# Sixteen expert items instead of seventeen: one item holds three experts

## The chip, the cores and the metric

One Trainium2 chip, one of its cores. A TensorE does matrix products of up to 128 x 128 weights against up to 512 columns; VectorE, ScalarE (ACT) and GpSimd (POOL) work on rows of 128 partitions; SyncE (SP) issues the loads of weights. The metric is the device time of one execution in microseconds (us), the median of several runs.

## The reference, cut to what matters

Two transformer blocks behind each other, for 512 tokens of 1024 values. The first has attention and a convolution, an output projection, and then a mixture of experts; the second (stick-breaking attention, gated linear attention, a gated mixer, a feed-forward layer) follows. The expert part is what changes:

```python
g_logits = hf @ w_rg + b_rg                    # 4 groups: top 1
e_logits = (hf @ w_re + b_re).reshape(T, 4, 8) # 8 experts in the group: top 2
eid = grp[:, None] * 8 + top_idx               # 512 tokens x 2 = 1024 assignments to 32 experts
y = (silu(x @ w_gate[e]) * (x @ w_up[e])) @ w_down[e]   # 1024 -> 512 -> 1024, fp32
out[token] += weight * y
```

All 32 experts' weights (6.3 MB each, 201 MB in all) have to be read; how many tokens an expert has depends on the data. The mixer of the second block ends in `mix @ w_o` with an RMS norm behind it (a sum of squares over 1024 channels), and the router stands behind another RMS norm.

## The kernel before, in words

**Expert items.** The experts are worked off in items of up to 128 token slots. An item's token rows are gathered by a product with a one-hot matrix (lines 1142 to 1195; `oh` on VectorE, `psg` on TensorE, high and low part of the rows, 64 products for two items at a time), then go through gate, up and down (`gate_up`, `down`), and a product with a second one-hot matrix adds the result to the tokens (`scatter`, line 1294). Fifteen items are pairs: two experts with 64 slots each, whose two products of 64 columns of weights run in the two halves of TensorE's array (`both`, line 1201). The expert with the most tokens (HOT) has an item to itself with 128 slots, and so has expert 31 (LAST). The list is `items = [*range(8), LAST, *range(8, NPR - 1), HOT, NPR - 1]`, 17 items. LAST is gathered by itself with 128 columns; HOT is gathered together with the pair at place 14. An expert with more tokens than slots would send the rest to a loop behind the items (line 1419), which runs as often as there are such blocks.

**Order.** From the second item on the order of TensorE's products is that of the program (`fixed`, line 1130). In each item: half of the gate, the transposes of the item before (`hidden_T`), half of the gather for the next two items where it is due, the second half of the gate, the down products of the item before, the second half of the gather, then up with the scatter of the item before in between (from line 1371 on). Before that, and around item 0, a scheduler places the instructions.

**The route.** Behind the router's logits VectorE finds each token's experts. `slots` (line 1048) counts the tokens of each expert, picks HOT and exchanges its place with that of expert 30, finds each assignment's slot (`sid`) and writes the list of experts by place (`ovf`). A table of tokens and weights by slot follows (`tsl`, `wsl`, by products `pstab`). Items 0 and 1 hold experts 0 to 3, whatever the data (`NFX = 4`), with slots found ahead of all this (`sid0`), so their gather and weights need not wait.

**Loads.** A stream issues loads of 1 MB on SyncE in the order of use, into 15 buffers in four pools; a load waits for its buffer. Of the pairs each load holds half for one and half for the other expert. From item 2 on SyncE reads the expert's number from `ovf` first.

**The other places.** The router (line 808) has in each of 8 steps a product for 36 logits and one for the sum of squares; both come between the output projection's products. Behind the items the second block's value projection starts; its weights are split in a high and a low part, the low part of the first two tiles by GpSimd (line 1458). The mixer's output projection (`mix_mm`, `mix_out`, lines 2170 to 2199) has 8 steps of two halves; the sum of squares over channels is a product with ones, one for each step and half (`Sums`, line 1630).

Of the kernel before, what the change touches and what calls it, by code (L numbers as in the profile page):

```python
# [11 lines left out]
F32 = mybir.dt.float32  # L12
# [8 lines left out]
P = 128  # L21
# [13 lines left out]
    ("b_mod", 48), ("g_norm1", 8), ("conv_b", 4), ("conv_ln_g", 4), ("conv_ln_b", 4),  # L35
    ("conv_w", 4 * 31), ("g_norm2", 8), ("w_router", 8 * 36), ("c", 8),
# [162 lines left out]
def _build(ctx, nc, tc, I, out, dbg):  # L199
# [108 lines left out]

    def mm3(ps, lh, ll, rh, rl, first, last):
# [39 lines left out]
    NPR, CAP, NFX = NE // 2 - 1, 64, 4  # L349
    HOT, LAST = NPR, NPR + 1  # L350
# [88 lines left out]
    def W(p, i):  # L439
# [3 lines left out]
        if p == LAST:  # L443
            return I["w_moe"][NE - 1, i]
        if p == HOT:
            return lambda: of(expert(2 * NPR), 1)
        if 2 * p < NFX:
# [3 lines left out]
    items = [*range(8), LAST, *range(8, NPR - 1), HOT, NPR - 1]  # L451

    def add_item(p, part):
        n = 2 if p >= NPR else 4
# [160 lines left out]
    with tc.issue_after(behind.ins):  # L615
# [6 lines left out]
        e64, base0, cand, isl, ish = [h2p.tile([P, NE], F32, name=n) for n in ("e64", "base0", "cand", "isl", "ish")]  # L622
        ts(e64, iota[:, :NE], 64.0, None, OP.mult)
        ts(isl, iota[:, :NE], float(NE - 1), None, OP.is_equal)
        ts(ish, iota[:, :NE], float(NE - 2), None, OP.is_equal)
        stt(base0, isl, 64.0, e64, OP.mult, OP.add)
        ts(cand, iota[:, :NE], NFX - 0.5, -1.0e5, OP.is_le, OP.mult)
        stt(cand, isl, -1.0e5, cand, OP.mult, OP.add)
# [174 lines left out]
    def router(st):  # L803
# [4 lines left out]
        mm(plg[0][0:36, :], wr(m), xs, start=(m == 0), stop=(m == KD - 1), skip_group_check=True)  # L808
        mm(plg[1][64:96, :], ones[:, 0:32], sq, start=(m == 0), stop=(m == KD - 1), skip_group_check=True)
# [146 lines left out]
    ovf = mp.tile([P, NOV + NE], I32, name="ovf")  # L956
# [91 lines left out]
    def slots():  # L1048
# [4 lines left out]
        key, hot, cap, base, ob, d, nb, g = [sm(NE) for _ in range(8)]  # L1053
        mx, at = sm(1), sm(1)
        stt(key, cn, float(NE), cand, OP.mult, OP.add)
        red(mx, key, axis=AX.X, op=OP.max)
        ts(hot, key, mx, None, OP.is_equal)
        tt(cap, hot, isl, OP.add)
        ts(cap, cap, float(CAP), float(CAP), OP.mult, OP.add)
        tt(ob, hot, base0, OP.mult)  # L1060
        nc.vector.reduce_sum(at, ob, axis=AX.X)
        ts(at, at, float(HOT * P), None, OP.subtract)
        stt(base, hot, float(HOT * P), base0, OP.mult, OP.add)
# [1319 lines left out]
```

## Time and profile before

| | |
|---|---|
| three timed runs | 1812.36, 1812.47, 1816.58 us (median 1812.47) |
| profiled execution | 1818.69 us, span 1816.9 us |
| TensorE busy | 1745.1 us (96%) |
| VectorE / ScalarE / GpSimd busy | 881.3 / 629.3 / 109.6 us |
| read from memory | 322.0 MB, 180 GB/s over the span |
| granted clock of TensorE, mean | 0.978 |

A profile shows one execution. Places in it are microseconds from the start of the span. "PE" is TensorE's products, "PEld" its loading of weights. Because products are pipelined, the difference between two starts tells what one costs, and its own duration is longer. fp32 products go in two passes and stand as two instructions.

### The profile page before, as it was taken

How to read it: one execution, taken by the hardware profiler on the slowest of the kernel's cores; microseconds unless marked ns; L12 is line 12 of the kernel's file. 1: busy time of each engine (PE TensorE's matmuls, PEld its weight loads, DVE VectorE, ACT ScalarE, POOL GpSimd, SP SyncE). 2: the span in 40 equal slices, each digit the busy share in tenths (PEclk: the TensorE clock that was granted, in tenths of full speed). 3: DMA queues.
4: the chain of work that ended last, by engine and by line, in shares of the span. 5: the costliest groups of instructions: out<-in, count | busy, mean ns of one | idle time of the engine just before them, and what ended most of it. 6: DMA issues, size and time to landing. Idle time of an engine off the chain costs nothing.

```text
span 1816.9 us, 26870 instructions
## 1 busy us (share of the span) xinstructions
PE 1745.1 (96%) x10826; PEld 1263.2 (70%) x10826; DVE 881.3 (49%) x1597; ACT 629.3 (35%) x1141; POOL 109.6 (6%) x147
## 2 busy tenths in 40 slices
PE   7999997999999999998899999999999999999997
PEld 4776565444445444445788668989999899789985
DVE  6789654433333334235577742253332645335534
ACT  5226653211111111104567743242233633223322
POOL 2000010000000000003200100030000111001101
PEclk9989898999999999999999999999999999999998
DMA  8563253999999999930411012113222222222221
GB/s 327 199 242 136 89 216 130 380 409 409 408 411 360 385 408 410 412 128 27 159 67 49 24 47 93 47 63 128 102 100 87 70 91 78 100 93 93 94 87 64
DMA packets 73986, 328.01 MB, mean 181 GB/s; under 512 B 8019, under 2 KB 8403, under 8 KB 59652
## 3 DMA queue, kind: packets, MB, share of 16 engines
q1 hardware_dynamic: 72608, 320.36, 46.6%
q0 software_dynamic: 1248, 5.91, 0.9%
q8 instruction: 86, 1.41, 0.3%
q14 instruction: 40, 0.33, 0.0%
q10 hardware_dynamic: 4, 0.00, 0.0%
HBM read 321.98 MB, written 4.26 MB: 180 GB/s over the span
## 4 chain that ended last, share of the span: by engine, by line
PE 48%; DVE 3%; ACT 2%; DMA 1%; POOL 1%; issue 1%; DVEq 0%; ACTq 0%; POOLq 0%
PE p L1620 11%; PE pup L2232 7%; PE pq L1598 4%; PE pg L312 2%; PE pg L310 2%; PE pg L311 2%; PE pd L311 2%; PE pd L312 2%; PE pd L310 2%; PE pv L310 1%; PE pv L311 1%; PE pv L312 1%; PE pmix L310 1%; PE psum L1643 1%; PE pmix L312 1%; PE pmix L311 1%
## 5 line engine op out<-in xcount | busy, mean ns | idle before, releaser
L224 DVE TENSOR_TENSOR wsplit<-raw,wsplit 128x1024 fp32r<-128x1024 f32 (+1 forms) x140 | 167.4, 1198 | 250.6 <-ACT wsplit L223 244.7
L223 ACT ACTIVATE wsplit<-raw 128x1024 fp32r<-128x1024 f32 (+1 forms) x144 | 146.8, 1022 | 260.5 <-PE pd L312 76.3
L1206 PE MATMUL pgu<-raw,x 128*64 128x512 f32 x960 | 220.3, 598 | 0.0
L1206 PEld LDWEIGHTS pgu<-raw,x 128*64 128x64 f32 x960 | 64.1, 136 | 119.9 <-issue 106.4
L1299 DVE SCALAR_TENSOR_TENSOR x<-psx,modc,x 128x512 f32<-128x512 f32 x136 | 93.2, 745 | 50.1 <-PE psx L1307 50.0
L1248 DVE SCALAR_TENSOR_TENSOR yl<-pdn,wsl,yh 128x512 fp32r<-128x512 f32 x34 | 25.4, 751 | 178.8 <-ACT yh L1247 178.3
L1206 PE MATMUL pdn<-raw,hT 128*64 128x512 f32 x480 | 105.7, 593 | 0.7 <-ACT hT L1228 0.7
L1228 ACT ACTIVATE hT<-pht 128x512 f32<-128x512 f32 x17 | 10.2, 597 | 232.0 <-PE pht L1222 227.5
L1206 PEld LDWEIGHTS pdn<-raw,hT 128*64 128x64 f32 x480 | 34.5, 137 | 69.1 <-issue 64.4
L647 DVE SCALAR_TENSOR_TENSOR y<-u,cpk,y 128x512 f32<-128x512 f32 x116 | 80.6, 748 | 0.1
L311 PE MATMUL pd<-wsplit,ah 128*128 128x512 f32 x176 | 71.1, 404 | 2.1 <-DVE wsplit L224 2.0
L1168 PE MATMUL psg<-oh,h2h 128*128 128x256 f32 (+1 forms) x288 | 67.8, 292 | 3.1 <-DVE oh L1153 3.1
L1620 PE MATMUL p<-nha,wsplit 128*128 128x258 f32 x384 | 69.0, 293 | 1.3 <-ACT wsplit L223 0.7
L312 PE MATMUL pd<-wsplit,al 128*128 128x512 f32 x176 | 70.1, 398 | 0.0
L310 PE MATMUL pd<-wsplit,ah 128*128 128x512 f32 x176 | 68.9, 397 | 0.9 <-ACT wsplit L223 0.9
L1168 PE MATMUL psg<-oh,h2l 128*128 128x256 f32 (+1 forms) x288 | 65.7, 282 | 0.0
L1620 PE MATMUL p<-nhb,wsplit 128*128 128x258 f32 x384 | 65.6, 283 | 0.0
L2232 PE MATMUL pup<-nha,wsplit 128*128 128x258 f32 x352 | 64.0, 291 | 0.4 <-ACT wsplit L223 0.4
L1306 PE MATMUL psx<-ohT,yh 128*128 128x512 f32 x136 | 59.3, 436 | 5.2 <-ACT wsplit L223 5.1
L2232 PE MATMUL pup<-nhb,wsplit 128*128 128x258 f32 x352 | 63.2, 287 | 0.0
L1168 PEld LDWEIGHTS psg<-oh,h2h 128*128 128x128 f32 x288 | 53.6, 196 | 9.7 <-issue 5.7
L1620 PEld LDWEIGHTS p<-nha,wsplit 128*128 128x128 f32 x384 | 56.2, 195 | 3.0 <-ACT wsplit L223 0.9
(653 smaller groups left out, 3973.5 us busy)
## 6 DMA issues: line engine op xcount, KB each, us to landing
raw<-w_moe SPq DMA_DIRECT2D x312, 512.0 KB, 10.1
raw<-w_moe SPq DMA_DIRECT2D x36, 1024.0 KB, 10.0
raw<-w_ff SPq DMA_DIRECT2D x22, 1024.0 KB, 4.8
raw<-w_mod SPq DMA_DIRECT2D x16, 1024.0 KB, 5.9
raw<-w_qk SPq DMA_DIRECT2D x12, 1024.0 KB, 5.1
raw<-w_v SPq DMA_DIRECT2D x8, 1024.0 KB, 4.9
raw<-w_modk SPq DMA_DIRECT2D x8, 1024.0 KB, 5.2
raw<-w_mg SPq DMA_DIRECT2D x8, 1024.0 KB, 4.9
```

The source lines that it names most:

```text
L223: act(hi, src, AF.Copy)
L224: return sub(lo, src, hi.bitcast(F32), OP.subtract)
L310: mm(ps, lh, rh, start=first, stop=False)
L311: mm(ps, lh, rl, start=False, stop=False)
L312: mm(ps, ll, rh, start=False, stop=last)
L647: tap[0] = stt(y[:, m, :], src, w, y[:, m, :], OP.mult, OP.add)
L1168: fix(mm(ps[k // 2][:, k % 2 * 256:][:, :n], w[i][:, k * P:(k + 1) * P], oh[:, i, :n], start=(i == 0 and w is h2h and k % 2 == 0), stop=(i ...
L1206: fix(mm(ps[s, :], l[:, s], w[:, 2 * b + i, :], start=first, stop=last, skip_group_check=True))
L1299: stt(xT[m], ps, gt2(m), xT[m], OP.mult, OP.add)
L1598: mm(ps[a], l[:, kk, :], r[kk][:, a * HF:(a + 1) * HF], start=(kk == 0 and fl == 0), stop=(kk == k - 1 and fl == 2))
L1620: mm(ps[a], l[:, kk, :], ends(r[kk])[:, a], start=(kk == 0 and fl == 0), stop=(kk == k - 1 and fl == 2))
L2232: mm(ps[:, a, :HC], l[:, kk, :], x[kk][:, o:o + HC], start=(kk == 0 and fl == 0), stop=(kk == KD - 1 and fl == 2))
```

## The change

The list has 16 items: 14 pairs, HOT, and an item TRI with three experts: one with 64 slots and the two emptiest (of those from expert 4 on) with 32 each. TRI's products are four of 32 columns, two of which belong to the expert with 64 slots (`three`); its loads are taken in threes (`several`). HOT and TRI stand one after the other in the middle of the list. `slots` now finds the two emptiest too, and exchanges three experts' places one after another (`trade`), and the list of experts by place is found from the places. With it came: the router's two products are 64 columns wide each (the columns of the packed constants are reordered so that 64 can be read), the low parts of the two value tiles go to VectorE, and in the mixer's projection the squares of six steps are added up on VectorE ahead of one product.

```diff
-    NPR, CAP, NFX = NE // 2 - 1, 64, 4
-    HOT, LAST = NPR, NPR + 1
+    NPR, CAP, NFX = NE // 2 - 2, 64, 4
+    HOT, TRI = NPR, NPR + 1
@@ W
+        if p == TRI:
+            e, i = 2 * NPR + 1 + i % 3, i // 3
+            return lambda: of(expert(e), 1)
-    items = [*range(8), LAST, *range(8, NPR - 1), HOT, NPR - 1]
+    items = [*range(8), HOT, TRI, *range(8, NPR)]
@@ router
-        mm(plg[0][0:36, :], wr(m), xs, start=(m == 0), stop=(m == KD - 1), skip_group_check=True)
-        mm(plg[1][64:96, :], ones[:, 0:32], sq, start=(m == 0), stop=(m == KD - 1), skip_group_check=True)
+        mm(plg[0][0:64, :], cc("w_router", 36 * m, 64), xs, start=(m == 0), stop=(m == KD - 1), skip_group_check=True)
+        mm(plg[1][64:128, :], ones[:, 0:64], sq, start=(m == 0), stop=(m == KD - 1), skip_group_check=True)
@@ slots
+        def best(oh, k):
+            mx = sm(1)
+            red(mx, k, axis=AX.X, op=OP.max)
+            ts(oh, k, mx, None, OP.is_equal)
+        def trade(oh, place):
+            at, to = sm(1), sm(1)
+            tt(t, oh, pos, OP.mult)
+            nc.vector.reduce_sum(at, t, axis=AX.X)
+            ts(at, at, float(place), None, OP.subtract)
+            ts(to, at, -1.0, None, OP.mult)
+            ts(t, pos, float(place), None, OP.is_equal)
+            stt(pos, t, at, pos, OP.mult, OP.add)
+            stt(pos, oh, to, pos, OP.mult, OP.add)
         stt(key, cn, float(NE), cand, OP.mult, OP.add)
+        best(hot, key)
+        stt(key, cn, -float(NE), cand, OP.mult, OP.add)
+        stt(key, hot, -1.0e5, key, OP.mult, OP.add)
+        best(c1, key)
+        stt(key, c1, -1.0e5, key, OP.mult, OP.add)
+        best(c2, key)
+        copy(pos, iota[:, :NE])
+        for oh_, place in ((hot, 2 * NPR), (c1, NE - 2), (c2, NE - 1)):
+            trade(oh_, place)
...
-        ts(eo[:, NOV + 1:], base[:, :NE - 1], 1.0 / 64, None, OP.mult)
+        for n, tag in enumerate(("hs", "hT")):
+            at = scratch(tag, DE, NE // 2, NE)
+            tt(at, iota[:, n * NE // 2:][:, :NE // 2, None].to_broadcast([P, NE // 2, NE]),
+               pos[:, None, :].to_broadcast([P, NE // 2, NE]), OP.is_equal)
+            tt(at, at, io(NE, NE // 2), OP.mult)
+            nc.vector.reduce_sum(eo[:, NOV + 1 + n * NE // 2:][:, :NE // 2], at, axis=AX.X)
@@ products
+    def three(ps, l, ws3, i, first, last):
+        for g in range(4):
+            s = slice(32 * g, 32 * g + 32)
+            fix(mm(ps[s, :], l[:, s], ws3[max(g - 1, 0)][:, i, :], start=first, stop=last, skip_group_check=True))
@@ gate_up (down is changed alike)
+            if p == TRI:
+                if k % 4 == 0:
+                    w = ws.several(3, 512)
+                three(ps, x[:, k, :], w, k % 4, k == 0, k == KD - 1)
@@ value projection
-    ws.pool, ws.rc, ws.rings, ws.lo = Halves(), 2, ws.rings[:1], nc.gpsimd.tensor_tensor
+    ws.pool, ws.rc, ws.rings, ws.lo = Halves(), 2, ws.rings[:1], tt
@@ mix_out
-        su.add(a, sqo[m])
+        if 0 < m < KD - 2:
+            tt(part(sqo[0], a), part(sqo[0], a), part(sqo[m], a), OP.add)
+        if m == 0 or m == KD - 2:
+            su.pend[a] = [sqo[0]] if m == 0 else su.pend[a] + [sqo[m]]
+        elif m == KD - 1:
+            su.add(a, sqo[m])
@@ for m in range(KD - 2)
             mix_mm(m, a)
-            su.flush(a)
```

## Rows read from the trace of the kernel before

**Rows 1.** Windows of the expert stage: busy (instructions) by engine, clock, DMA share, GB/s
```profile
545.00:633.00 88.00, 88.00 (x411) 45.11 (x411) 33.06 (x69) 13.59 (x28) 0.00 (x0) 1.00 0.96 372
633.00:755.00 122.00, 122.00 (x607) 55.83 (x604) 44.16 (x85) 16.15 (x32) 0.00 (x0) 1.00 1.02 409
755.00:816.00 61.00, 60.25 (x228) 26.20 (x226) 19.51 (x30) 5.73 (x9) 0.00 (x0) 1.00 0.56 212
```
**Rows 2.** Timeline of TensorE (start, length, what), LAST's item: gate half, scatter half
```profile
545.46 3.60 PE L1214 MATMUL pgu<-raw,x 128*128 128x512 f32 x8
548.90 0.60 PE L1222 MATMUL pht<-ident,hs 128*128 128x128 f32 x4
...
596.59 0.50 PE L1306 MATMUL psx<-ohT,yh 128*128 128x512 f32 x1
...
598.64 3.65 PE L1206 MATMUL pgu<-raw,x 128*64 128x512 f32 x16
```
**Rows 3.** Timeline of TensorE: first product behind the expert stage
```profile
821.34 0.72 PE L1306 MATMUL psx<-ohT,yh 128*128 128x512 f32 x1 [5.06 <-ACT wsplit L223]
```
**Rows 4.** Groups of TensorE by shape, 500 to 546 us: gather of one item
```profile
L1168 PE MATMUL psg<-oh,h2h 128*128 128x128 f32 x32 | 7.3, 277 | 0.0
```
**Rows 5.** Timeline of TensorE: products of 32 columns, four such rows each
```profile
831.91 0.62 PE L1276 MATMUL pss<-sq,ones 128*32 128x512 f32 x1
...
832.36 0.59 PE L1276 MATMUL pss<-sq,ones 128*32 128x512 f32 x1
```
**Rows 6.** Timeline of VectorE: the route
```profile
316.07 0.19 DVE L1055 SCALAR_TENSOR_TENSOR r<-pcn,cand 128x32 f32<-128x32 f32 x1 [0.56 <-PE pcn L1052]
316.30 0.19 DVE L1056 TENSOR_REDUCE r<-r 128x1 f32<-128x32 f32 x1
...
316.93 0.19 DVE L1058 TENSOR_TENSOR r<-r,isl 128x32 f32<-128x32 f32 x1
317.04 0.19 DVE L1060 TENSOR_TENSOR r<-r,base 128x32 f32<-128x32 f32 x1
...
320.22 0.65 DVE L1083 TENSOR_TENSOR hs<-iota,r 128x480 f32<-128x480 f32 x1
...
326.35 0.17 DVE L1104 TENSOR_SCALAR r<-r 128x4 f32<-128x4 f32 x1 [2.05 <-ACT r L1103]
...
337.44 0.88 DVE L1153 SCALAR_TENSOR_TENSOR oh<-iota,sp,oh 128x256 fp32r<-128x256 f32 x2
```
**Rows 7.** Timeline of TensorE: first product of the gather for item 2
```profile
338.26 0.36 PE L1168 MATMUL psg<-oh,h2h 128*128 128x256 f32 x1
```
**Rows 8.** Window behind the wait of rows 3
```profile
821.50:824.80 3.30, 3.30 (x8) 1.93 (x8) 1.72 (x3) 1.50 (x3) 1.43 (x2) 0.50 0.46 194
```
**Rows 9.** Timeline of SyncE: first loads that need an expert's number
```profile
327.77 9.32 SPq L270 DMA_DIRECT2D raw<-w_moe  x8
```
**Rows 10.** Timeline of TensorE: a step of the router, one of eight
```profile
252.15 1.05 PE L808 MATMUL plg<-xs,cpk 128*36 128x512 f32 x2
253.12 1.04 PE L809 MATMUL plq<-sq,ones 128*32 128x512 f32 x2
254.10 0.66 PE L817 MATMUL pth<-ident,xs 128*128 128x128 f32 x4
```
**Rows 11.** Timeline of TensorE: mixer's projection, from one sum to the next
```profile
1367.26 0.60 PE L1643 MATMUL psum<-sq,ones 128*128 128x260 f32 x2
...
1367.82 0.28 PE L311 MATMUL pmix<-mla,wsplit 128*128 128x256 f32 x1
1367.94 0.28 PE L312 MATMUL pmix<-mha,wsplit 128*128 128x256 f32 x1
...
1370.54 0.59 PE L1643 MATMUL psum<-sq,ones 128*128 128x256 f32 x2
```
**Rows 12.** Line 224 by engine: low parts of weights, ns min/median/max, first and last
```profile
L224 DVE TENSOR_TENSOR wsplit<-raw,wsplit x140: 683/1226/2324, 871.5 to 1797.8; 128x1024 fp32r<-128x1024 f32 x128, 128x512 fp32r<-128x512 f32 x12
...
L224 POOL TENSOR_TENSOR wsplit<-raw,wsplit x4: 2377/2392/2402, 823.7 to 847.0; 128x1024 fp32r<-128x1024 f32 x4
```

More of the change, by code (lines that the diff above doesn't have):

```diff
@@ L307, in nxt, with several @@
             return r.rearrange("p (k n) -> p k n", n=n)
+        def several(self, m, n):
+            self.load()
+            self.cast(self.i + max(m, self.rc - 1))
+            r = [self.got.pop(self.i + j).rearrange("p (k n) -> p k n", n=n) for j in range(m)]
+            self.i += m
+            return r
     def mm3(ps, lh, ll, rh, rl, first, last):
@@ L449, in W @@
         return lambda: [of(expert(2 * p + b), 2) for b in range(2)]
-    items = [*range(8), LAST, *range(8, NPR - 1), HOT, NPR - 1]
+    items = [*range(8), HOT, TRI, *range(8, NPR)]
     def add_item(p, part):
-        n = 2 if p >= NPR else 4
+        n = {HOT: 2, TRI: 6}.get(p, 4)
         for i in range(n * part, n * part + n):
@@ L955, in _build @@
     ovb = mp.tile([P, NOV], F32, name="ovb")
-    ovf = mp.tile([P, NOV + NE], I32, name="ovf")
+    ovf = mp.tile([P, NOV + 1 + NE], I32, name="ovf")
     sid0 = rp.tile([P, 2, 4], F32, name="sid0")
@@ L1229, in hidden, with down @@
         return t
-    def down(t, psd, one=False):
+    def down(t, psd, p=None):
+        one = p == HOT
         for k in range(4):
+            if p == TRI:
+                if k % 2 == 0:
+                    w = ws.several(3, 512)
+                for n in range(2):
+                    three(psd[n], t[:, k, :], w, k % 2 * 2 + n, k == 0, k == 3)
+                    yield
+                continue
             if k % 2 == 0 or not one:
@@ L1323, in start_gather @@
     def start_gather(p, sid, banks=()):
-        n = 2 if p < LAST else 1
+        n = 2
         x, g = gather(float(p * P), n, sid, banks)
@@ L1342, in pick @@
     def pick(p):
-        n = 2 if p < LAST else 1
+        n = 2
         x = [ep.tile([P, KD, P], F32, name="x", tag="x", bufs=3) for _ in range(n)]
@@ L1374, in _build @@
         fixed[0] = at > 0
-        single, rest = p >= NPR, None
+        rest = None
         if q is not None:
@@ L1381, in _build @@
         pg[p] = pgu("pgu")
-        g = gate_up(xs[p], pg[p], single)
+        g = gate_up(xs[p], pg[p], p)
         steps(g, 4)
@@ L1394, in _build @@
             psd = [pdn("pdn"), pdn("pdn")]
-            steps(down(t, psd, q >= NPR), 8)
+            steps(down(t, psd, q), 8)
             o = slots_T(tsl[:, q:q + 1])
@@ L1400, in _build @@
         pu[p] = pgu("pgu")
-        g = gate_up(xs[p], pu[p], single)
+        g = gate_up(xs[p], pu[p], p)
         for _ in range(2):
@@ L1431, in _build @@
         for h in range(2):
-            run(gate_up(x, pgo[h], True))
+            run(gate_up(x, pgo[h], HOT))
         ho = ep.tile([P, DE], F32, name="hs", tag="hs", bufs=1)
@@ L1437, in _build @@
         pdo = [pdn("pdn"), pdn("pdn")]
-        run(down(t, pdo, True))
+        run(down(t, pdo, HOT))
         run(scatter(weighted(pdo, cols[:, 2:3], True), slots_T(cols[:, 1:2], True), pms))
@@ L1639, in add, with flush @@
             self.pend[a].append(sq)
-        def flush(self, a):
+        def flush(self, a, last=True):
             for sq in self.pend[a]:
-                mm(self.ps[a], ones, part(sq, a), start=(self.n[a] == 0), stop=(self.n[a] == KD - 1))
+                mm(self.ps[a], ones, part(sq, a), start=(self.n[a] == 0), stop=last)
                 self.n[a] += 1
@@ L2172, in mix_mm @@
             wo[m] = ws.nxt(P)
-            sqo[m] = t5("sq")
+            sqo[m] = t5("sq") if m else HP.tile([P, L], F32, name="sqs", tag="rstd2", bufs=2)
         wh, wl = wo[m]
@@ L2194, in _build @@
             mix_mm(m, a)
-            su.flush(a)
+            su.flush(a, False)
             mix_out(m, a)
@@ L2217, in h_gen @@
             act(part(sq, a), h, AF.Square)
-            su.flush(a)
+            su.flush(a, False)
             su.add(a, sq)
```

40 lines of the change are left out of this document (17 added, 23 removed).

## The prediction, made before the result was known

> **What bounds the kernel now.** I read the page first: TensorE is busy for nearly the whole span (the table above), so the question in each stretch is whether it works without a gap or waits. The change touches four stretches: the output projection with the router (244 to 297 us), the expert stage (314 to 816), the value projection behind it (816 to 862) and the mixer's last projection (1366 to 1406). The windows view then gives TensorE and DMA together [rows 1]: in the expert stage TensorE shows hardly a gap and the granted clock is full, while the weights arrive at 409 GB/s in the stretch from 633 to 755. So two limits lie close together. The timeline decides between them: between 545 and 633 only 372 GB/s moved, because the buffers were full and the loads waited for TensorE, and after 755 they again came at TensorE's pace. TensorE is therefore the limit and the loads have a little room. How much: from 545 on, 372 x 88 + 409 x 122 + 212 x 61 = 95.6 MB were moved [rows 1]. At 409 GB/s throughout that is 234 us, so loading alone could end near 779. With the last load's arithmetic (half of 3.44 us, [rows 2]) the stage can't end before some 781 us. It ends now at 816.3 (the wait of 5.06 us ahead of the row at 821.34, [rows 3]). No saving in the stage can exceed 35 us, whatever TensorE is spared.
>
> **The expert stage, items.** A pair item and the old single last item cost TensorE the same: both stream 512 columns 24 times, twice for fp32. What goes is one such item whole. Half a gate takes 548.90 - 545.46 = 3.44 us, and there are six such halves in gate, up and down (20.6); the four transposes 0.6; half of its scatter 598.64 - 596.59 = 2.05, twice (4.1) [rows 2]. The old last item also had a gather of its own: 32 products of the high and 32 of the low part with 128 columns, in alternation, 7.3 us [rows 4]. In the new list the hot expert's item and the three-expert item share one ordinary gather, so this goes too. Sum: 20.6 + 0.6 + 4.1 + 7.3 = 32.6 us less.
>
> **The three-expert item itself.** It issues four products of 32 columns where a pair issues two of 64: 48 groups of four (24 steps, two passes each) instead of 48 of two. Four products of 32 columns side by side stand in this trace at line 1276: four start within 0.02 us of 831.91 and the next four at 832.36, so a group takes 0.45 us [rows 5], against 3.44 / 8 = 0.43 for a step of the single item. I take 48 x 0.02 = 1.0 us more. The bounds: nothing (the streamed columns are the same), and 48 x 0.43 = 20.6 if only two ran at a time. A rule speaks against it: the Trainium skill, "TensorE: Matmul & The Clock Gate", section "Measured speedup vs the span model", lists less than the full factor for packed products, 3.07 times for four row tiles and 2.38 for three column tiles. By 3.07 a group would take 4 / 3.07 = 1.30 passes, an estimate of some 6 us more for the item and a forecast later by 5; the row of this trace has 0.45 us and decides.
>
> **The route, which pays for it.** Which experts are hot and which two are emptiest, and the exchange of their places, are found on VectorE in a chain of small operations. There were 11 between the counts and the bases; there are 39 now. Their starts are between 0.11 us (317.04 - 316.93, two that don't depend on each other) and 0.23 us (316.30 - 316.07, dependent) apart, so 28 more cost 3.1 to 6.4 us; most depend on the one before, and I take 4.5. The list of experts by place adds six operations of 512 elements, each like the 480-element one at 320.22 (0.65 us): 3.9 us. Of this, 2 us can lie in the idle time of 2.05 us that VectorE has ahead of 326.35, while it waits for an exponential [rows 6]. So everything behind it on VectorE's queue is some 6.4 us later: the slot table, the product that closes item 0, and the one-hot rows of the gather for item 2. Who waits for that: TensorE transposes item 0's hidden rows and then takes the gather for item 2 from 338.26 on, and the last one-hot rows are done only at 337.44 + 0.88 (two merged) = 338.3 [rows 6, 7]. There is 0.6 us to spare, since the fourth tile's products come last. TensorE's order is fixed there, so nothing passes the waiting product. I take a new wait of 6 us. Its second price is the clock: behind the wait of 5.06 us at 821.34 the granted clock was 0.50 (1.2 GHz) from 821.5 to 824.8 [rows 3, 8], which costs half of 3.3 us. Together 7.5 us; bounds 1 us (the added work falls into VectorE's other gaps) and 12 (all dependent, nothing hidden).
>
> **The loads in this place.** SyncE issues in order and the first load that needs an expert's number goes out at 327.77, right behind the fixed ones [rows 9]. The numbers will come some 8 us later than now, so loads stop for about 6 us, with some still under way. If TensorE waits in the same place, the buffers ahead of it stay full and nothing is lost; without that wait, up to 4 us. Cost taken: none, bound 4. The three-expert item needs its loads in threes (18.9 MB in all, 46 us at 409 GB/s, where TensorE works under 30), but the hot expert's item ahead of it only a third of that (15 us): the two together are what two pairs are.
>
> **Router products.** Each of 8 steps has the logits (36 columns) and the sum of squares (32 columns) one behind the other: 252.15, 253.12, and the next work at 254.10, 1.95 us [rows 10]. Both become 64 columns wide, in the two halves of the array, as the pairs of the experts are. They should then cost what one does: 0.97 us less, eight times, 7.8 us. TensorE has no gap between these steps, and the last pair feeds the logits' copy directly, so I count it whole. Bounds: 0, and 7.8.
>
> **Sums of squares in the mixer's projection.** 16 become 6; ten additions of 260 columns go to VectorE. Two sums stand 1370.54 - 1367.26 = 3.28 us apart, and 24 matrix products between them at 0.12 (1367.94 - 1367.82) make 2.88, so a sum costs 0.40 us with its change of weights [rows 11]: ten are 4.0 us. They lie between products without a gap, and each addition has 3 us until it is needed. Bounds 2.5 (the pass alone, 0.25) and 4.
>
> **The rest at nothing.** The low parts of two weight tiles move from GpSimd (2.4 us each) to VectorE (1.2) behind the expert stage [rows 12]. TensorE there is held by VectorE's updates of x; four more operations on that queue may delay these by as much as the earlier low parts bring. Zero, bounds -2 and +2. Five constants less on VectorE, the reordered columns and one table column less are worth nothing: TensorE doesn't wait there.
>
> **The sum.** -32.6 + 1.0 + 7.5 in the expert stage (-24.1), -7.8, -4.0: -35.9 us. The profiled execution took 1818.7 us (span 1816.9 and 1.8 around it) and would take 1782.8. The three timed runs have a median of 1812.5, 6 us below the profiled one, so the same difference gives 1776.6, put as 1776.
>
> **The rivals.**
> 1. The route hides. VectorE has gaps while it waits for ACT and TensorE; if the additions fall into them, the 7.5 us shrink to 1 and loads decide: 1770. Against it: the chain's operations depend on each other, and the gather's rows are just in time now.
> 2. The loads become the limit. Late numbers, a wait at the start and three loads for one step could leave TensorE waiting for weights at the end of the list, as six pairs in a row need 30.8 us of loading each (12.6 MB at 409 GB/s) against 25.3 of work and half of a gather (7.3 / 2). With 8 us of such waits beside the 4.5 more of the route's upper bound, 1788.
> 3. The narrow products gain nothing in one of the places: two at a time in the three-expert item, +20 us (1796), or the router's pair in turn, +8 (1784). Against it: rows 5. For it: products of 36 and 32 columns in different parts of the array ran one behind the other [rows 10].
> 4. Slower: the three-expert item's four products run one after another. Place: its 48 groups; price: 48 x (4 x 0.43 - 0.45) = 61 us, 1837. It decides from 0.45 + 36 / 48 = 1.2 us a group on. The same rows 10 speak for it, rows 5 against.
> 5. It doesn't do what it says: if an expert overflows its slots, the loop behind the items runs a pass. By the reference's own routing on its inputs the fullest expert has 108 tokens (128 slots), the two emptiest that may be chosen 9 and 14 (32), and all others at most 56 (64), so it runs no pass, as before.
>
> **How the numbers follow.** Forecast (the wait of 4 to 10 us, everything else as summed) 0.53; rival 1 0.17; rival 2 0.18; rival 3 0.08; rival 4 0.03; rival 5 0.01. Likeliest 1776. With eight in ten: 1766, where the stage gains all 35 us that the loads leave it and the rest comes as summed, to 1790, where rival 2 or the router's part of rival 3 holds. A measurement of this kernel tells 0.3% (5.4 us) from no change. All cases but rivals 4 and 5 are faster by more than that, and nothing lies near no change: faster 0.95, same 0.01, slower 0.04.
>
> **What would show it.** In the profile after: sixteen groups of hidden transposes instead of seventeen and no gather with 128 columns; the three-expert products in groups of four 0.45 us apart; the logits and squares starting together, eight steps of about 1 us; six sums in the mixer instead of sixteen; a wait of TensorE for VectorE near 330 (8 us earlier than now) ahead of the transposes or the second gather, and half the clock behind it; DMA near 409 GB/s up to the end of the list. The forecast is wrong if TensorE waits for weights for more than 5 us, if the wait for the route is under 2 or over 12, or if groups of four are over 0.5 us apart.

## The result, and the profile after

The changed kernel takes 1771.8 us (median of 4 runs, 1764.9 to 1774.7), the kernel before 1812.4 in the same comparison (1810.0 to 1816.6): a ratio of 0.9765, 95% interval 0.9743 to 0.9787, 40.6 us less. The forecast was 1776. The profiled execution took 1770.8 us (span 1769.0), 47.9 less than that of before; some seven microseconds lie between the two differences, and the first and the seventh line of the table below hold 6.9 of them.

The table cuts both spans at places that the timelines of TensorE show (first products of a kind, and the end of the last down product), so that a stage is the time from one to the next. In the rows `pgu` are products of gate and up, `pdn` of down, `pht` the transposes of hidden rows, `psg` the gather, `psx` the scatter and `pstab` the slot table.

| from ... to | before | after | difference | forecast |
|---|---|---|---|---|
| start to the first router product | 252.1 | 247.3 | -4.8 | 0 |
| router: to the first gather product | 54.2 | 46.9 | -7.3 | -7.8 |
| route and item 0: to the first hidden transposes | 31.5 | 41.0 | +9.5 | +7.5 |
| items: to the end of the last down product | 478.4 | 445.1 | -33.3 | -31.6 |
| behind the items: to the first query product | 55.5 | 51.3 | -4.2 | 0 |
| query projection: to its last product | 145.5 | 143.7 | -1.8 | 0 |
| to the mixer's first product | 341.4 | 339.3 | -2.1 | 0 |
| mixer: to the feed-forward's first product | 52.5 | 48.3 | -4.2 | -4.0 |
| to the end of the last down product of the layer | 394.6 | 394.6 | 0.0 | 0 |

The first line needs no work of the change, as the fourth experiment shows; nor does the line ahead of the mixer, a stretch that took from 336.7 to 342.5 us in kernels that are alike there. Without these two the sum is -41.3 us, close to the difference of the medians.

**The items.** The windows of the expert stage, with the columns of [rows 1]: TensorE has no gap up to 755 us, and the loads now run at 404 to 409 GB/s there, so what room they had is nearly used.

```profile
543.00:634.00 91.00, 91.00 (x501) 42.35 (x500) 33.81 (x65) 11.44 (x22) 0.00 (x0) 1.00 1.01 404
634.00:755.00 121.00, 121.00 (x596) 53.88 (x597) 40.82 (x74) 16.55 (x33) 0.00 (x0) 1.00 1.03 409
755.00:780.00 25.00, 24.25 (x112) 9.91 (x108) 8.00 (x12) 1.97 (x3) 0.00 (x0) 1.00 0.88 351
```

The timeline of TensorE in HOT and the three-expert item (start, length, what), answering to [rows 2, 5]. A half of HOT's gate takes 546.41 - 542.98 = 3.43 us; a half of the three-expert item's, 32 products of 32 columns, 571.72 - 568.15 = 3.57, eight groups of four at 0.446 us.

```profile
542.98 3.60 PE L1263 MATMUL pgu<-raw,x 128*128 128x512 f32 x8
546.41 0.60 PE L1271 MATMUL pht<-ident,hs 128*128 128x128 f32 x4
...
568.15 3.64 PE L1248 MATMUL pgu<-raw,x 128*32 128x512 f32 x32
571.72 0.55 PE L1271 MATMUL pht<-ident,hs 128*128 128x128 f32 x3
```

**The route.** The timeline of TensorE where it meets the route; the bracket is the idle time ahead and what ended it. The gather for item 2 (the last row) answers to [rows 7]. TensorE stands still in front of the products for the slot table, 5.77 and 0.85 us, and not in front of the gather.

```profile
308.04 11.38 PE L1242 MATMUL pgu<-raw,x 128*64 128x512 f32 x52
325.19 1.99 PE L1158 MATMUL pstab<-hs,po 128*128 128x93 f32 x8 [5.77 <-DVE hs L1154]
328.03 2.02 PE L1158 MATMUL pstab<-hT,po 128*128 128x93 f32 x8 [0.85 <-DVE hT L1154]
329.97 5.33 PE L1242 MATMUL pgu<-raw,x 128*64 128x512 f32 x16
335.23 0.66 PE L1271 MATMUL pht<-ident,hs 128*128 128x128 f32 x4
335.64 0.36 PE L1204 MATMUL psg<-oh,h2h 128*128 128x256 f32 x1
```

The windows around it: half the clock (1.2 GHz) from 326 to 330 and for a part of the time up to 336, as behind the wait of [rows 8]. The half gate at 329.97 takes 5.26 us up to the transposes instead of 3.58 as in later items. In the last column the loads fall to 83 GB/s: SyncE's next load waits 9.8 us there for a buffer that TensorE's gate products still read.

```profile
326.00:330.00 4.00, 3.15 (x16) 2.75 (x15) 3.23 (x13) 1.88 (x2) 0.00 (x0) 0.50 1.02 372
330.00:336.00 6.00, 6.00 (x24) 2.17 (x24) 3.14 (x12) 0.03 (x1) 0.00 (x0) 0.72 0.31 83
```

VectorE's timeline there, answering to [rows 6]: the search begins at 304.81 and the slots (`sid`) are ready at 319.80, 15.0 us, where it was 316.07 to 323.97. One of the six wide operations is the 0.69 us at 311.17; each of the six pushes the next start 0.58 to 0.61 us back, 3.6 together, so that some 3.5 of the 7.1 us more are the small operations (an estimate by difference). The idle time ahead of the exponential is still there, 2.38 us.

```profile
304.81 0.19 DVE L1079 SCALAR_TENSOR_TENSOR r<-pcn,cand 128x32 f32<-128x32 f32 x1 [0.56 <-PE pcn L1059]
...
311.17 0.69 DVE L1114 TENSOR_TENSOR hT<-iota,r 128x512 f32<-128x512 f32 x1
...
319.38 0.42 DVE L1046 TENSOR_REDUCE sid<-s 128x8 f32<-128x256 f32 x1
...
322.52 0.17 DVE L1140 TENSOR_SCALAR r<-r 128x4 f32<-128x4 f32 x1 [2.38 <-ACT r L1139]
```

**The other places.** A router step, answering to [rows 10]: logits and squares start together, and from one step's start to the next work it is 279.87 - 278.86 = 1.01 us instead of 1.95.

```profile
278.86 0.64 PE L815 MATMUL plg<-xs,cpk 128*64 128x512 f32 x1
278.86 0.64 PE L816 MATMUL plq<-sq,ones 128*64 128x512 f32 x1
279.34 0.59 PE L815 MATMUL plg<-xs,cpk 128*64 128x512 f32 x1
279.87 0.66 PE L824 MATMUL pth<-ident,xs 128*128 128x128 f32 x4
```

Behind the items the last scatter starts 2.94 us after TensorE's last product, and is released by a branch of VectorE's queue; before, it waited 5.06 for ScalarE's split of the first value weights [rows 3]. The low parts (line 224, [rows 12]) are now all on VectorE and begin at 785.6 there.

```profile
783.28 0.50 PE L1363 MATMUL psx<-ohT,yh 128*128 128x512 f32 x1 [2.94 <-DVEq L1476]
```

### The profile page after: what moved, and what is told of

Its sections match the earlier page's. It is cut to its first block, busy times and chain, and to the rows that moved or that the text cites. A ratio compares the mean times of both kernels' runs of the same rounds, so it can differ in the third digit from the quotient of the medians.

```text
span 1769.0 us, 26743 instructions
## 1 busy us (share of the span) xinstructions
PE 1692.4 (96%) x10770; PEld 1235.4 (70%) x10770; DVE 878.8 (50%) x1615; ACT 624.6 (35%) x1133; POOL 102.8 (6%) x143
## 4 chain that ended last, share of the span: by engine, by line
PE 49%; DVE 4%; ACT 2%; POOL 1%; issue 0%; DVEq 0%; POOLq 0%
PE p L1677 11%; PE pup L2293 7%; PE pq L1655 5%; PE pg L320 2%; PE pg L318 2%; PE pg L319 2%; PE pd L319 2%; PE pd L320 2%; PE pd L318 2%; PE pv L318 1%; PE pv L320 1%; PE pv L319 1%; PE pmix L318 1%; PE pmix L320 1%; PE pmix L319 1%; PE psb L1948 1%
## 5 line engine op out<-in xcount | busy, mean ns | idle before, releaser
L224 DVE TENSOR_TENSOR wsplit<-raw,wsplit 128x1024 fp32r<-128x1024 f32 (+1 forms) x144 | 171.6, 1194 | 230.1 <-ACT wsplit L223 223.7
L1242 PE MATMUL pgu<-raw,x 128*64 128x512 f32 x896 | 206.0, 602 | 0.0
L1242 PEld LDWEIGHTS pgu<-raw,x 128*64 128x64 f32 x896 | 60.4, 137 | 113.6 <-issue 102.5
L1356 DVE SCALAR_TENSOR_TENSOR x<-psx,modc,x 128x512 f32<-128x512 f32 x128 | 87.7, 745 | 44.5 <-PE psx L1364 42.8
L1242 PE MATMUL pdn<-raw,hT 128*64 128x512 f32 x448 | 98.7, 593 | 0.7 <-ACT hT L1277 0.7
L1204 PE MATMUL psg<-oh,h2h 128*128 128x256 f32 x256 | 60.9, 298 | 3.2 <-DVE oh L1189 3.2
L1363 PE MATMUL psx<-ohT,yh 128*128 128x512 f32 x128 | 54.9, 429 | 3.2 <-DVEq L1476 2.9
L1204 PE MATMUL psg<-oh,h2l 128*128 128x256 f32 x256 | 57.7, 281 | 0.0
L1677 PEld LDWEIGHTS p<-nhb,wsplit 128*128 128x128 f32 x384 | 54.5, 190 | 0.0
```

The costliest lines, as they stand in the source:

```text
L224: return sub(lo, src, hi.bitcast(F32), OP.subtract)
L1204: fix(mm(ps[k // 2][:, k % 2 * 256:][:, :n], w[i][:, k * P:(k + 1) * P], oh[:, i, :n], start=(i == 0 and w is h2h and k % 2 == 0), stop=(i ...
L1242: fix(mm(ps[s, :], l[:, s], w[:, 2 * b + i, :], start=first, stop=last, skip_group_check=True))
L1356: stt(xT[m], ps, gt2(m), xT[m], OP.mult, OP.add)
L1677: mm(ps[a], l[:, kk, :], ends(r[kk])[:, a], start=(kk == 0 and fl == 0), stop=(kk == k - 1 and fl == 2))
```

## The experiments

The stage lengths of the experiments, cut as above; "route" is the stage with item 0.

| kernel (experiment) | router | route | items | behind | query | mixer | median us |
|---|---|---|---|---|---|---|---|
| changed | 46.9 | 41.0 | 445.1 | 51.3 | 143.7 | 48.3 | 1771.8 |
| expert change alone (1) | 54.2 | 40.0 | 445.1 | 53.2 | 145.1 | 52.5 | 1785.6 |
| places as constants (2) | 46.9 | 32.4 | 445.1 | 52.0 | 145.3 | 48.3 | 1762.7 |
| lists by swaps (3) | 47.1 | 41.4 | 445.1 | 51.2 | 143.8 | 48.3 | 1772.9 |
| before, no last item (4) | 54.2 | 31.9 | 446.0 | 56.1 | 145.6 | 52.5 | 1781.1 |
| router 64 and 32 (5) | 54.4 | 40.7 | 445.2 | 51.2 | 143.8 | 48.3 | 1778.7 |
| swaps in the gaps (6) | 47.0 | 33.6 | 445.9 | 51.3 | 143.7 | 48.3 | 1765.9 |
| table late (7) | 46.9 | 36.3 | 446.6 | 51.4 | 143.7 | 48.2 | 1765.4 |
| both (8) | 46.9 | 36.7 | 446.3 | 51.2 | 143.9 | 48.3 | 1769.9 |
| changed again (9) | 46.9 | 41.2 | 445.2 | 51.3 | 143.7 | 48.3 | 1771.5 |
| swaps in the gaps again (10) | 47.0 | 35.2 | 445.1 | 51.2 | 143.3 | 48.3 | 1766.4 |
| low parts on GpSimd (11) | 46.9 | 40.8 | 445.1 | 53.1 | 144.8 | 48.3 | 1772.7 |

The medians come from four comparisons, in which the kernel before itself took 1812.4, 1814.3 (experiments 1 to 4), 1814.5 (5 to 8) and 1816.9 us (9 to 11). A difference of a few microseconds between kernels of different comparisons is therefore read from the stages.

**1. The expert change alone.** The order of the constants, the router's products, the mixer's sums and the low parts are put back.

```diff
-        mm(plg[0][0:64, :], cc("w_router", 36 * m, 64), xs, ...)
-        mm(plg[1][64:128, :], ones[:, 0:64], sq, ...)
+        mm(plg[0][0:36, :], wr(m), xs, ...)
+        mm(plg[1][64:96, :], ones[:, 0:32], sq, ...)
...
-    ws.pool, ws.rc, ws.rings, ws.lo = Halves(), 2, ws.rings[:1], tt
+    ws.pool, ws.rc, ws.rings, ws.lo = Halves(), 2, ws.rings[:1], nc.gpsimd.tensor_tensor
...
-        if 0 < m < KD - 2:
-            tt(part(sqo[0], a), part(sqo[0], a), part(sqo[m], a), OP.add)
...
+        su.add(a, sqo[m])
```

> The expert change alone: the router products, the order of the constants, the mixer's sums and the low parts are as before the change. Theory (the parts add up, each in its own stage): the expert stage keeps what it gained, 33 us less in the items against 8.7 us more in the route, about 24 us in all, so 1788 us against 1812; in the trace the router stage, the step from the last expert to the value projection and the mixer stand as before (0 us gained in each, where the changed kernel has -7.3, -2.8 and -4.3). Rival 1 (the parts meet: an earlier route or a later one eats what the router products give): the expert stage gains over 4 us more or less than 24. Rival 2 (the 4.8 us that the attention stage gained come from the order of the constants): the attention stage is as before here; if it gains about 5 us again although nothing of it is changed, they are a difference between runs.

Measured: 1785.6 us, ratio 0.9829 (0.9801 to 0.9858), 28.7 less than before. Router and mixer are as before, to a tenth; items and route together are 24.8 us shorter. So the parts add up by stage, and rival 1 is out, but the sum left out 2.3 us behind the items, which come with the expert change: the last scatter starts 2.94 us after the last down product here too, with the low parts where they were. Which of its edits moved that start was not found out. The attention stage is as before in this profile, so taken alone it would speak for rival 2; the fourth decides that.

**2. Places as constants.** The search, the trades and the list by place are made at set-up, for the experts that these inputs give; what is left out of the kernel is finding them from the data.

```diff
-        key, hot, c1, c2, pos, cap, base, t, d, nb, g = [sm(NE) for _ in range(11)]
-        ...
-        for oh_, place in ((hot, 2 * NPR), (c1, NE - 2), (c2, NE - 1)):
-            trade(oh_, place)
-        ...
+        d, nb, g = [sm(NE) for _ in range(3)]
...
+        copy(eo[:, NOV + 1:], inv)
```

> The changed kernel with the places of the experts, their slots and the list of experts by place as constants made during set-up: the search for the fullest and the two emptiest experts, the three trades and the six wide operations are left out. Theory (the route is a wait of TensorE and nothing covers it): the 5.8 and 0.8 us for which TensorE waits ahead of the slot table are gone and the first item's products run at the full clock, so 8 to 9 us less than the changed kernel, about 1763 us. Rival 1 (the loads of the expert weights take over as the limit once the route is short): a wait for weights of over 3 us shows in the expert stage and the gain is under 5 us. Rival 2 (the stall ahead of the exponential holds the table by itself): a wait of 2 us or more stays ahead of the slot table and the gain is 5 to 6 us.

Measured: 1762.7 us, ratio 0.9697 (0.9664 to 0.9729), 9.1 less than the changed kernel; against the kernel before it is 51.6 less where the changed kernel is 40.6. The route stage is 8.6 us shorter and within 0.9 of before. TensorE's waits from 327 to 780 us (waiting line, for what: us in all, times, longest) name no weights, so rival 1 is out. The slot table's first product starts at 317.15 behind work of item 0 and without a wait, although VectorE still sits idle for 2.18 us ahead of the exponential, so rival 2 is out too. So the route's price is a wait and nothing takes its place.

```profile
PE psx L1334 <- ACT uh L1494: 3.0, 1, 3.0
PE pdn L1213 <- ACT hT L1248: 0.7, 1, 0.7
PE psx L1334 <- DVE x L1327: 0.5, 1, 0.5
```

**3. Exponentials ahead, the list by swaps, both lists behind the slots.**

```diff
+            tc.keep_in_program_order(tt(u, oh, iota[:, :NE], OP.mult))
+            nc.vector.reduce_sum(e, u, axis=AX.X)
+            ts(u, iota[:, :NE], at, None, OP.is_equal)
+            tt(at, v, e, OP.subtract)
+            stt(inv, u, at, inv, OP.mult, OP.add)
+            copy(v, e)
...
-        for n, tag in enumerate(("hs", "hT")):
-            at = scratch(tag, DE, NE // 2, NE)
-            ...
+        for s in swaps:
+            swap(*s)
...
-        slots()
...
         act(ge, gd, AF.Exp)
...
         act(ex, ex, AF.Exp)
...
+        slots()
```

> The changed kernel with the same places, but the exponentials of the gate weights are asked for ahead of the search, the list of experts by place is made by three swaps of narrow operations instead of six wide ones, and both lists stand behind the slots. Theory (TensorE waits for VectorE's chain, so whatever leaves the chain comes back): the exponential's 2.4 us stall, 4.1 us of wide operations less 2.3 us of narrow ones and 0.6 us of small ones leave the chain, the table's first product comes about 5 us earlier, the wait falls from 5.8 to about 1 us, and the time by 4 to 6 us, about 1767 us. Rival 1 (the chain is bound by latency between dependent narrow operations, not by the wide ones): the narrow swaps cost as much as the six wide operations and the gain is under 3 us. Rival 2 (the exponential ahead delays the evictions of the gather on the scalar engine): the gather's products end later by 1 us or more and the gain is lost.

Measured: 1772.9 us, ratio 0.9761 (0.9732 to 0.9789): no gain, rival 1 was right. VectorE's timeline shows why. The slots are ready at 317.49, 2.3 us earlier, but then nearly every operation of a swap needs the one before and starts 0.19 to 0.29 us behind it; the three swaps take from 317.40 to 321.20, the second list 1.7 and the gate weights 1.0 us more, and the table starts no earlier: TensorE waits 5.9 us for it.

```profile
317.07 0.42 DVE L1046 TENSOR_REDUCE sid<-s 128x8 f32<-128x256 f32 x1
317.40 0.18 DVE L1075 TENSOR_TENSOR r<-r,iota 128x32 f32<-128x32 f32 x1
317.62 0.18 DVE L1076 TENSOR_REDUCE r<-r 128x1 f32<-128x32 f32 x1
317.84 0.24 DVE L1077 TENSOR_SCALAR r<-iota,r 128x32 f32<-128x32 f32 x1
318.12 0.16 DVE L1078 TENSOR_TENSOR r<-r,r 128x1 f32<-128x1 f32 x1
```

**4. The kernel before without its last item.** Expert 31's tokens get nothing from it here.

```diff
-    items = [*range(8), LAST, *range(8, NPR - 1), HOT, NPR - 1]
+    items = [*range(8), *range(8, NPR - 1), HOT, NPR - 1]
```

> The kernel before with the item of the last expert left out (its tokens get nothing from it), and nothing else changed. Theory (an item costs its products, its transposes, its scatter and its own gather, all on TensorE): 32.6 us less, about 1780 us, with the route as before. Rival (part of the item is hidden: the loads or the gather of the next pair set the pace there): 20 to 25 us less, and a wait of TensorE for weights of over 3 us turns up.

Measured: 1781.1 us, ratio 0.9817 (0.9788 to 0.9845), 33.1 less; the item stage 32.4 less. The theory holds. This kernel is that of before up to the items, and still its first router product comes 6.1 us earlier. From 176 to 189.4 us the starts behind TensorE's waits agree to 0.02 us in the two. The windows from 188 to 206 us, of before and then of this kernel, show TensorE at 0.56 and at 1.00 of the clock: the attention stage differs between executions of the same code. The kernel of the first experiment, with the order of the constants put back, has 0.58 there and 252.6 us. All ten profiles with the new order of the constants lie between 245.8 and 248.3; whether that order makes the long stretch at half clock rarer was not tested.

```profile
188.00:206.00 18.00, 16.58 (x71) 9.01 (x72) 11.54 (x35) 11.24 (x32) 0.00 (x0) 0.56 0.00 1
```

```profile
188.00:206.00 18.00, 14.71 (x101) 8.77 (x101) 16.56 (x48) 15.80 (x46) 0.00 (x0) 1.00 0.00 1
```

**5. The router's pair with 64 and 32 columns.**

```diff
-        mm(plg[1][64:128, :], ones[:, 0:64], sq, ...)
+        mm(plg[1][64:96, :], ones[:, 0:32], sq, ...)
```

> The changed kernel with the product for the row sums put back to 32 columns (of ones, at column 64), while the product for the logits keeps its 64 columns. Before the change the two had 36 and 32 columns and started 0.97 us after each other; with 64 and 64 they start together. Theory A (36 columns are what keeps the pair apart, the widths need not be equal): 64 and 32 start together too, the router stage stays 7.3 us shorter than before the change, time as the changed kernel, 1772 us. Theory B (two products ride together only with equal widths): they run in turn again, the stage gives back about 7 us, 1779 us.

Measured: 1778.7 us, ratio 0.9803 (0.9776 to 0.983). Theory B: in the timeline of TensorE the second product starts 1.00 us behind the first, and the stage is back at 54.4. Of the three pairs of widths seen in the router (36 and 32, 64 and 64, 64 and 32) only the equal one starts together.

```profile
247.82 1.07 PE L815 MATMUL plg<-xs,cpk 128*64 128x512 f32 x2
248.82 1.05 PE L816 MATMUL plq<-sq,ones 128*32 128x512 f32 x2
```

**6. The swaps in the gaps.** As the third, but nothing is held behind the slots.

```diff
-            tc.keep_in_program_order(tt(u, oh, iota[:, :NE], OP.mult))
+            tt(u, oh, iota[:, :NE], OP.mult)
...
-        tc.keep_in_program_order(nc.vector.reduce_sum(pg, ge, axis=AX.X))
+        nc.vector.reduce_sum(pg, ge, axis=AX.X)
```

> As the kernel with the lists by swaps (exponentials ahead, list of experts by three swaps), but the swaps and the rest of the gate weights are not held behind the slots: they may stand between the steps of the search and the trades. Theory (the chain is bound by the 0.2 us from one narrow operation to the next that needs its result; an operation that needs nothing of it fits in between for about nothing): the slots are ready at 317 to 318 us of the profile, nothing but the table follows, its first product comes at about 320 us instead of 325, the wait of TensorE falls from 5.8 to under 1.5 us, and the time by 5 to 7 us against the changed kernel, about 1766 us. Rival (what counts is the sum of VectorE's operations, 0.1 us and more for each wherever it stands): the 24 more narrow operations cost 2.4 us of chain again, the slots come after 319 us and the gain is under 4 us.

Measured: 1765.9 us, ratio 0.9729 (0.9705 to 0.9753). The route stage is 7.4 us shorter. The timeline of VectorE, and then that of TensorE: the swaps' operations (lines 1077 and 1078) stand between steps of the trades, 0.06 to 0.16 us apart, and cost the chain about nothing. From the search's start (305.41) to the slots (317.79) it is 12.4 us with everything in it, where the third experiment had 12.1 and 6.4 more behind. The table's first product waits for nothing, its second half 1.28 us.

```profile
305.41 0.19 DVE L1096 SCALAR_TENSOR_TENSOR r<-pcn,cand 128x32 f32<-128x32 f32 x1 [1.50 <-PE pcn L1059]
...
310.85 0.15 DVE L1090 TENSOR_SCALAR r<-r 128x1 f32<-128x1 f32 x1
310.91 0.23 DVE L1077 TENSOR_SCALAR r<-iota,r 128x32 f32<-128x32 f32 x1
311.06 0.14 DVE L1091 TENSOR_SCALAR r<-r 128x1 f32<-128x1 f32 x1
311.12 0.24 DVE L1093 SCALAR_TENSOR_TENSOR r<-r,r,r 128x32 f32<-128x32 f32 x1
311.28 0.15 DVE L1078 TENSOR_TENSOR r<-r,r 128x1 f32<-128x1 f32 x1
...
317.37 0.42 DVE L1046 TENSOR_REDUCE sid<-s 128x8 f32<-128x256 f32 x1
```

```profile
320.00 1.30 PE L1171 MATMUL pstab<-hs,po 128*128 128x93 f32 x8
322.58 1.30 PE L1171 MATMUL pstab<-hT,po 128*128 128x93 f32 x8 [1.28 <-DVE hT L1167]
323.81 3.65 PE L1255 MATMUL pgu<-raw,x 128*64 128x512 f32 x16
```

**7. The table late.** The route as in the changed kernel; the table's first half has a buffer of its own, and the table stands behind half of item 1's gate.

```diff
-            vv = scratch(("hs", "hT")[k], DE, 4, 3, NB)
+            vv = (scratch("hT", DE, 4, 3, NB) if k else
+                  rp.tile([P, 12 * NB], F32, name="vv", tag="vv", bufs=1)...)
...
         steps(g, 4)
+        if at == 1:
+            tables(wk)
```

> The changed kernel with its route as it is, but the work for the slot table has a buffer of its own for its first half (not the one in which item 0's hidden rows are put), and stands behind the first half of item 1's gate products and the one-hot rows of the next gather. Theory (TensorE stands still only because item 1's gate waits for item 0's hidden rows, whose buffer the table holds): item 1's gate starts when item 0's products end, at about 319.4 us of the profile, covers 3.5 us of the wait, the gather of the next pair starts at 329 to 331 us instead of 335.6, and the time falls by 5 to 6 us, about 1766 us. Rival (the gate waits for something else, a weight or an accumulator): item 1's gate starts no earlier than 328 us and nothing is gained.

Measured: 1765.4 us, ratio 0.9725 (0.9699 to 0.975). The gate does start at 320.98 and covers part of the wait, so it was held by the buffer and not by weights, but 2.34 and 1.01 us of waiting stay, because on VectorE the table now comes behind the gather's one-hot rows. The gather started at 332.1, a microsecond later than the 329 to 331 expected. The route stage gains 4.7 us and the items give back 1.5, 3.2 together, while the medians say 6.4; the rest is within what the spread of the runs (1761.8 to 1769.3) leaves open.

```profile
320.98 3.65 PE L1247 MATMUL pgu<-raw,x 128*64 128x512 f32 x16 [0.61 <-ACT hs L1456]
326.98 1.58 PE L1163 MATMUL pstab<-vv,po 128*128 128x93 f32 x8 [2.34 <-DVE vv L1159]
329.56 2.01 PE L1163 MATMUL pstab<-hT,po 128*128 128x93 f32 x8 [1.01 <-DVE hT L1159]
```

**8. Both.** The edits of 6 and 7 together, with one `po` buffer less (2 for 3).

> Both of the last two together: the shorter chain (exponentials ahead, list by swaps in the gaps) and the table behind the first half of item 1's gate. Theory: slots at about 317.5 us, no wait or one under 1.5 us is left, the gather of the next pair starts at 327 to 328 us instead of 335.6, 8 us less than the changed kernel, about 1764 us, as much as leaving the search out gave. Rival (the gains overlap, since both cover the same wait): not over 2 us better than the better of the two.

Measured: 1769.9 us, ratio 0.9734 (0.9708 to 0.9761): no better than either. The table's products come at 326.5, about as in 7 (327.0), although the slots are ready 1.9 us earlier (318.80 against 320.75): on VectorE the table stands behind the one-hot rows and these behind item 0's hidden rows, which start at 321.2 and 321.0, and the shorter chain in front gains nothing there. The gains overlap, as the rival said.

**9 to 11. Repeats, and the low parts on GpSimd.** The changed kernel and the kernel of 6 once more, without an edit, and

```diff
-    ws.pool, ws.rc, ws.rings, ws.lo = Halves(), 2, ws.rings[:1], tt
+    ws.pool, ws.rc, ws.rings, ws.lo = Halves(), 2, ws.rings[:1], nc.gpsimd.tensor_tensor
```

> The changed kernel once more, beside the next two on the same chip. Theory (the 4.8 us that the attention stage gained in its first profile, 138 to 206 us, are the granted clock of that execution and not the change): the profile may show the stage with or without a stretch at half clock; router stage 7.3 us shorter, route 8 to 9 us dearer, items 33 us shorter, mixer 4.3 us shorter as before; median 1770 to 1774 us.

> The kernel with the exponentials ahead and the list by swaps in the gaps once more, to compare it with the changed kernel on the same chip. Theory (the wait of TensorE ahead of the slot table is 6 to 8 us shorter): 5 to 8 us faster than the changed kernel in the same rounds. Rival (the first comparison, 1765.9 against 1771.8 us, was within what runs differ): under 3 us.

> The changed kernel with the low parts of the second block's weights back on GpSimd. Theory (VectorE makes them earlier and TensorE's value and query projections wait less): of what the changed kernel gained behind the experts, the 1.4 us between the last expert and the value projection and up to 1.7 us in the query projection are given back, 1.5 to 3 us in the profile, about 1774 us. Rival (those gains come from where the last item ends): they stay, and the time is the changed kernel's to within 1 us.

Measured on one chip: 1771.5 us (ratio 0.9749, 0.9728 to 0.977), 1766.4 (0.9719, 0.9694 to 0.9744) and 1772.7 (0.9762, 0.9742 to 0.9783). The changed kernel repeats in every stage of this table to 0.2 us; its start to the first router product is 248.3 us (247.3 in the first profile). The kernel of 6 is 5.1 us better again; the intervals overlap, but the route stage, 6.0 us shorter, says the same. Its two profiles have 33.6 and 35.2 us there: in the second the clock fell behind the same wait of 1.3 us (0.76 of full from 322 to 326, 0.81 from 326 to 330, where the first shows 1.00) and the half gate took 4.44 us instead of 3.59. This kernel and that with the table late (experiment 7, 1765.4) are the fastest here that compute everything; the runs do not tell the two apart. With the low parts on GpSimd 1.8 us come back behind the items and 1.1 in the query projection, 2.9 in the profile; the medians differ by 1.3, within what they can tell. TensorE's waits show where: 1.2 us for VectorE's `dg`, of which the changed kernel has none, and 1.7 instead of 0.6 for ScalarE's `sqk` in the query projection.

```profile
810.23 1.10 PE L1586 MATMUL pspread<-dg,ones 128*128 128x512 f32 x2 [1.22 <-DVE dg L1583]
```

## Why the prediction was right, point by point

**The bound.** Right: TensorE is the limit in the expert stage, before and after; with the route 9 us shorter (experiment 2) the items still take 445.1 us without a wait for weights. The ceiling of 35 us that the loads were to set stays untested: no run gained more than 32.4 us in route and items together (experiment 2).

**Items, -32.6.** Experiment 4 measures the item alone at -32.4.

**Three-expert item, +1.0.** The groups stand 0.446 us apart, as foreseen (0.45). But the items as a whole lost 33.3, so this item costs 0.9 less than nothing: it was compared with the single item (3.43 for a half), while what it replaces in the list is a pair, whose half takes 3.59 (323.81 to the transposes at 327.40 in experiment 6) against its 3.57. The forecast had taken pair and single item for equal. That explains zero. Of the last 0.9 some 0.6 lie in the gathers, whose halves take 3.91 and 3.94 us here and 3.98 and 4.00 in experiment 4; why, and the rest, stays open. Two profiles of one kernel differ by as much (445.9 and 445.1, experiments 6 and 10). The Trainium skill, "TensorE: Matmul & The Clock Gate", section "Measured speedup vs the span model", would by its 3.07 have given 1.30 passes or 0.56 us a group, an estimate; the trace does not bear it out for this shape.

**Route, +7.5.** The mechanism was right, the size 2.0 too small and the place wrong. The stage lost 9.5 us, of which 8.6 go with the search (experiment 2). The slots were to be 6.4 us later and are 7.1, but the parts were not as summed: nothing was hidden, where 2 were taken off, and the small operations cost some 3.5 instead of 4.5. That the sum came so near is in part luck. The forecast had TensorE wait at the transposes and the gather; the products of the slot table stand ahead of these in its queue, and there it waited 6.6 us (forecast 6). The half clock behind it cost 1.7 us in the half gate and 0.7 in the table's second products (1.94 us to the next work, 1.23 in experiment 6), 2.4 where 1.5 were taken; the last 0.5 of the 9.5 is not placed. The step "2 us can lie in the idle time" failed: the idle time did not shrink (2.38 us, 2.05 before), because it begins only when the chain has ended. ScalarE's timeline shows what it is, two loads of a function table of 1.28 us each. The first is a preload that line 1505 asks for ahead of the second block; it stands between the two exponentials, and the second of these loads its own table again behind it:

```profile
319.01 0.22 ACT L1135 ACTIVATE r<-r 128x16 f32<-128x16 f32 x1 [8.40 <-DVE r L1134]
319.70 1.28 ACT L1505 ACT_TABLE_LOAD   x1 [0.47 <-PE pgu L1242]
320.99 1.28 ACT L1139 ACT_TABLE_LOAD   x1
322.28 0.20 ACT L1139 ACTIVATE r<-r 128x4 f32<-128x4 f32 x1
```

The Trainium skill, "ScalarE activation tables: per-element evaluation and per-set limits", section "What a function is on this engine", puts one such load at 1283 ns; the trace agrees.

**Loads, 0.** Right: SyncE issued no load between 314.7 and 320.4 us, about the 6 us foreseen, and no wait for weights came of it.

**Router, -7.8.** -7.3: a step takes 1.01 us where 0.98 was foreseen (1.95 - 0.97). **Mixer, -4.0.** -4.2, a little beyond the bound of 4; the sums' products fall from 64 to 44, two for each sum.

**The rest at nothing.** Here the sum was short. The low parts bring 2.9 us in the profile (experiment 11), just past the bound of 2, by shorter waits of TensorE for VectorE and ScalarE and not by its updates of x, where the forecast looked; a further 2.1 us (5.06 - 2.94) come from the last scatter's earlier start, which no step looked at; 0.3 behind the items and 0.7 in the query projection stay open.

**The sum.** -35.9 was forecast, -41.3 is there: -6.0 behind the items (with the query projection), -1.7 in the items, +2.0 in the route, +0.5 in the router and -0.2 in the mixer make the difference of -5.4. The route's error hid a third of what was missed behind the items, which is luck. Of the likeliest case the wait came true, between 4 and 10 us; "everything else as summed" did not hold behind the items.

**The rivals.** The route did not hide (1); had it, loads would not have decided, as experiment 2 shows at 1763 us without a wait for weights. No wait for weights came (2). The router's half of rival 3 was nearer than it looked: one of the two left at 32 columns brings it about (experiment 5). Four in turn (4) is out by the rows above (0.446 us a group); and the transposes come in sixteen groups, and no gather with 128 columns, as a pass of the loop would need, is in the trace (5).

## What to carry to other kernels

A stage in which the bound engine has no gap gave back what it was spared (32.4 us of the 32.6 summed), and could be summed from the durations of its own products. Small work added on another engine was priced by the chain that it lengthens and by the first thing on the bound engine's queue that needs the end of that chain, which had to be looked up in the queue's order; here that was a table nobody needs for another item, ahead of work that was ready. Before such a chain is shortened, its steps' distances tell whether work can be put into its gaps instead of behind it: here the same work cost 6.4 us behind and about nothing inside.

## What the runs showed of the hardware

Two products side by side in TensorE's columns start together when both are 64 wide (0.48 us for the pair and pass) and four when all are 32 wide (0.446), but 36 with 32 and 64 with 32 ran one behind the other, 0.97 to 1.00 us each with its two passes. No other widths were tried.

On VectorE operations of up to 32 elements that need each other's result start 0.19 to 0.29 us apart in experiment 3, others in experiment 6 from 0.05 to 0.16. The same 18 operations of the swaps, the second list and the gate weights cost 6.4 us behind the chain and about 0.3 inside it (12.4 against 12.1).

The granted clock of the attention stage differs between executions of the same code: 0.56 of full from 188 to 206 us in the profile of before, 1.00 in that of experiment 4, and the time to the first router product is 6.1 us shorter. Behind a wait of 1.3 us in the route it stayed full in one profile of the kernel of experiment 6 and fell in the other (experiment 10).
